# One hybrid decoder layer on one core: the second MLP product as seven block products instead of eight

## The chip, the core and the metric

The kernel runs on one core of one Trainium2 chip. The metric is the device time of one execution in microseconds (us), the median of several runs. Shorter is better.

## What is computed

One decoder layer over 2048 tokens of width 1024, in float32: an RMS norm, one input projection into three head groups (a gated causal convolution, a retention in chunks of 128 tokens, and dilated sliding-window attention), an output projection onto the residual, and an MLP. The change is in the MLP:

```python
x = x + mix.astype(x.dtype)
h2 = rms_norm(x, norm2_g)
ff = jnp.square(jax.nn.relu(h2 @ w_ff1.astype(F32))) @ w_ff2.astype(F32)
return x + ff.astype(x.dtype)
```

`w_ff1` is 1024 x 4096 and `w_ff2` 4096 x 1024. "The first MLP product" below is `h2 @ w_ff1`, "the second" the product with `w_ff2`.

## The kernel before

Everything is held transposed, channels on the 128 partitions and tokens along the free axis. The precision of float32 is kept by splitting each operand into a rounded part and a remainder: `halves` copies a 128x512 block into the rounded format on ScalarE and subtracts that from the original on VectorE. `mm3` then issues three matmuls of 128x512 for a pair of operands (rounded with rounded, rounded with remainder, remainder with rounded). Each operand lives in a unit of 4 KB per partition, from a pool with a fixed number of units: `wcp` (6, weights), `actp` (8, activations), `ur` (24), `ul` (8). Raw blocks land in `stage` (3 buffers).

The program's stages, by the time of the profiled execution: first projections with convolution and retention, then the attention's projections (to some 650 us); attention (to 920); output projection (to 1134); then the MLP twice, for tokens 0 to 1023 (H = 0, to 1808) and 1024 to 2047 (H = 1).

**First MLP product.** For each of 16 pairs of hidden rows (`pair`), seven block products of 12 matmuls each replace the eight that a 2 x 2 block product has (Winograd's form of Strassen's scheme: sums of weight blocks on GpSimd, `weight_sums`; sums of activation blocks on VectorE, made once; the block products collected in two PSUM banks and by VectorE). `pair` ends in the squared ReLU, two VectorE instructions of 128x1024, and two stores to `hid_d` in device memory.

**Second MLP product.** `group(g)` runs eight times per half, each over four hidden rows of 128: it loads four blocks of hidden and four of `w_ff2` (512 KB each) and splits them; then for each of 8 output blocks `d` and 2 token blocks `c` it sums 12 matmuls in one PSUM bank (`pso`), and VectorE adds the bank to `acc`. That is 8 x 16 x 12 = 1536 matmuls per half. While H = 0 does this, the operands of H = 1 for the first product are prepared (`next_half`).

**Order.** The program is written out in a nominal order, and a scheduler plays it through ahead of time and sets the order in which each engine's queue holds its instructions; an engine works its queue strictly in that order. Loads and stores go from SyncE's queue (SP), apart from the stores of the output projection, which go from GpSimd's (POOL).

**Around the change's other place**, the first projections: `conv_part(i)` and `retain(i)` for each 128-token chunk i give the matmuls. On GpSimd run the inverse roots (`rsqrt`: `rstd` per chunk, `rrr` per head, `rc` in the convolution), the gate product `rg` and `ro`, the retention's output times that gate. The path from a chunk's retention to PE goes: `rss` (VectorE), `rrr` (GpSimd), `rrr` x decay and `ro` (VectorE), `ro` x gate (GpSimd), transposes `ptr` (PE). The convolution's 31 taps are 248 VectorE instructions over 128x512 (`conv_chunk`), spread between these. GpSimd does nothing with `w_ff2` in this kernel.

## Time and profile before

| | |
|---|---|
| runs | 2489.5, 2485.09, 2488.97 us; median 2488.97 |
| profiled execution, its own time | 2485.31 us |
| span from first to last instruction | 2483.5 us |
| busy: PE, VectorE, ScalarE, GpSimd | 98%, 60%, 35%, 20% of the span |
| instructions: PE matmuls, VectorE, ScalarE, GpSimd | 12062, 2888, 1987, 363 |
| moved by DMA | 287.34 MB, mean 116 GB/s |
| chain that ended last | PE 88%, DVE 5%, DMA 3% |

PE is TensorE, DVE VectorE, ACT ScalarE, POOL GpSimd, SP SyncE's queue. Where an engine's busy time in a stretch equals the stretch, nothing on it waits there; a matmul's length in the profile overlaps the next one's, so the spacing of matmuls is the length of a stretch divided by their count. The chain of waits says the same in another way: it is followed back from the last instruction, and the engine that holds most of it sets the time.

### The profile page before, as it was taken

How to read it: one execution, taken by the hardware profiler on the slowest of the kernel's cores; microseconds unless marked ns; L12 is line 12 of the kernel's file. 1: busy time of each engine (PE TensorE's matmuls, PEld its weight loads, DVE VectorE, ACT ScalarE, POOL GpSimd, SP SyncE). 2: the span in 40 equal slices, each digit the busy share in tenths (PEclk: the TensorE clock that was granted, in tenths of full speed). 3: DMA queues.
4: the chain of work that ended last, by engine and by line, in shares of the span. 5: the costliest groups of instructions: out<-in, count | busy, mean ns of one | idle time of the engine just before them, and what ended most of it. 6: DMA issues, size and time to landing. Idle time of an engine off the chain costs nothing.

```text
span 2483.5 us, 32837 instructions
## 1 busy us (share of the span) xinstructions
PE 2434.3 (98%) x12062; PEld 2019.5 (81%) x12062; DVE 1478.2 (60%) x2888; ACT 873.0 (35%) x1987; POOL 504.1 (20%) x363
## 2 busy tenths in 40 slices
PE   7999999999999999999999999999999999999999
PEld 7878888999877776878888888888878888888887
DVE  5586787764476865675655565445575556644542
ACT  6433325333566674443222322112142223321210
POOL 0232211233122423344222200000132321000000
PEclk9999999999898999999999999999999999999999
DMA  7422104342352538552323363243132223632311
GB/s 217 133 64 73 38 19 117 95 115 84 97 107 77 115 84 286 188 179 101 126 103 110 111 229 124 80 152 111 68 114 107 102 104 134 234 106 68 119 68 68
DMA packets 192014, 287.34 MB, mean 116 GB/s; under 512 B 40317, under 2 KB 129516, under 8 KB 191852
## 3 DMA queue, kind: packets, MB, share of 16 engines
q1 hardware_dynamic: 189292, 276.85, 34.9%
q0 software_dynamic: 2560, 8.39, 0.9%
q8 instruction: 95, 1.56, 0.3%
q14 instruction: 67, 0.55, 0.1%
HBM read 213.19 MB, written 71.99 MB: 115 GB/s over the span
## 4 chain that ended last, share of the span: by engine, by line
PE 88%; DVE 5%; DMA 3%; ACT 1%; issue 1%; POOL 1%; SPq 0%; ACTq 0%; DVEq 0%; POOLq 0%
PE pso L917 29%; PE ps L158 16%; PE psy L917 11%; PE psz L917 7%; PE psx L917 7%; PE psc L917 6%; PE po L712 2%; PE sp L665 2%; PE pt L691 2%; PE sp L666 2%; DMA xn<-x 1%; PE rsp L350 1%; PE rpo L365 1%; DMA xs<-xT 1%; PE pb L167 1%
## 5 line engine op out<-in xcount | busy, mean ns | idle before, releaser
L917 PE MATMUL pso<-hid,w2a 128*128 128x512 f32 x1536 | 361.6, 395 | 0.0
L917 PE MATMUL pso<-hid,w2b 128*128 128x512 f32 x1536 | 361.1, 395 | 0.0
L917 PEld LDWEIGHTS pso<-hid,w2b 128*128 128x128 f32 x1536 | 288.0, 188 | 70.2
L917 PEld LDWEIGHTS pso<-hid,w2a 128*128 128x128 f32 x1536 | 288.0, 188 | 70.2
L929 DVE TENSOR_TENSOR acc<-acc,pso 128x512 f32<-128x512 f32 x256 | 174.4, 684 | 275.9 <-PE pso L917 275.3
L158 PE MATMUL ps<-whi,hh 128*128 128x384 f32 (+1 forms) x896 | 313.4, 351 | 12.5 <-ACT whi L117 9.4
L158 PE MATMUL ps<-whi,hl 128*128 128x384 f32 (+1 forms) x896 | 314.8, 351 | 0.3 <-DVE hl L150 0.3
L158 PE MATMUL ps<-wlo,hh 128*128 128x384 f32 (+1 forms) x896 | 311.8, 348 | 0.0
L929 POOL TENSOR_TENSOR s<-w1raw 128x512 f32<-128x512 f32 x64 | 93.8, 1485 | 758.3 <-DMA w1raw<-w_ff 693.0
L917 PE MATMUL psy<-T,S 128*128 128x512 f32 x768 | 192.4, 396 | 0.6 <-DVE S L619 0.5
L917 PE MATMUL psx<-B,A 128*128 128x512 f32 x768 | 191.8, 395 | 0.0
L158 PEld LDWEIGHTS ps<-whi,hh 128*128 128x128 f32 x896 | 169.3, 189 | 24.1 <-ACT whi L117 9.4
L158 PEld LDWEIGHTS ps<-whi,hl 128*128 128x128 f32 x896 | 169.3, 189 | 12.0 <-issue 5.4
L158 PEld LDWEIGHTS ps<-wlo,hh 128*128 128x128 f32 x896 | 169.3, 189 | 9.6 <-issue 3.1
L217 DVE SCALAR_TENSOR_TENSOR acc<-cbuf,cwt,acc 128x512 f32<-128x512 f32 x240 | 175.4, 776 | 0.2
L917 PEld LDWEIGHTS psy<-T,S 128*128 128x128 f32 x768 | 143.9, 188 | 36.2 <-DVE S L619 1.0
L917 PEld LDWEIGHTS psx<-B,A 128*128 128x128 f32 x768 | 144.1, 188 | 34.8
L917 PE MATMUL psc<-mix,wohi 128*128 128x512 f32 x512 | 164.0, 401 | 5.1 <-ACT wohi L641 2.7
L619 DVE TENSOR_TENSOR S<-s,S 128x512 fp32r<-128x512 f32 x128 | 109.2, 857 | 68.7 <-ACT S L617 68.1
L676 ACT ACTIVATE lt<-lt,ml 128x256 f32<-128x256 f32 (+1 forms) x288 | 129.2, 452 | 28.8 <-DVE ml L673 28.2
L617 ACT ACTIVATE S<-s 128x512 fp32r<-128x512 f32 x128 | 79.9, 628 | 164.1 <-PE psy L917 96.6
L617 ACT ACTIVATE hid<-hidraw 128x512 fp32r<-128x512 f32 x128 | 74.3, 626 | 164.6 <-DMA hidraw<-hid_d 116.2
(188 smaller groups left out, 3914.9 us busy)
## 6 DMA issues: line engine op xcount, KB each, us to landing
w1raw<-w_ff SPq DMA_DIRECT2D x66, 512.0 KB, 3.3
hidraw<-hid_d SPq DMA_DIRECT2D x64, 512.0 KB, 4.3
w2raw<-w_ff SPq DMA_DIRECT2D x64, 512.0 KB, 3.3
woraw<-w_out SPq DMA_DIRECT2D x33, 512.0 KB, 4.2
hid_d<-hidB SPq DMA_DIRECT2D x32, 512.0 KB, 2.7
hid_d<-hidA SPq DMA_DIRECT2D x32, 512.0 KB, 2.7
xs<-xT SPq DMA_DIRECT2D x31, 512.0 KB, 4.1
qkraw<-qkT_d SPq DMA_DIRECT2D x48, 256.0 KB, 4.8
```

The lines of the kernel that those rows point to most:

```text
L158: nc.tensor.matmul(ps, a[:, k, :], b[k][:], start=(k == 0 and m == 0), stop=(k == KT - 1 and m == 2))
L167: nc.tensor.matmul(pb[:, :TW], rb[:, h0 + u:h0 + u + 1].to_broadcast([33, P]), bands[:], start=True, stop=True)
L217: nc.vector.scalar_tensor_tensor(out=accs[j], in0=src, scalar=cwt[:, j, w:w + 1], in1=accs[j], op0=ALU.mult, op1=ALU.add)
L617: nc.scalar.activation(out=u[:, 0, :], in_=raw, func=AF.Copy)
L619: sub.tensor_tensor(out=u[:, 1, :], in0=raw, in1=u[:, 0, :].bitcast(F32), op=ALU.subtract)
L665: nc.tensor.matmul(sp[:, c0:c0 + n], qs[h][:, qsl], khi[h][:, ksl], start=True, stop=False)
L666: nc.tensor.matmul(sp[:, c0:c0 + n], qs[h][:, qsl], klo[h][:, ksl], start=False, stop=True)
L676: last_exp[0] = nc.scalar.activation(out=lt[:, :n], in_=lt[:, :n], func=AF.Exp, scale=-1.0, bias=mls[u][:, h:h + 1], accum_out=mls[u][:, 2 ...
L691: nc.tensor.transpose(pts[u][:, q * P:(q + 1) * P], lts[h, u][:, c * P:(c + 1) * P], ident[:])
L712: nc.tensor.matmul(po[h * 64:(h + 1) * 64, u0 * P:(u0 + n) * P], vt[:, kv, h * 64:(h + 1) * 64], mv, start=(one or i == 0), stop=(one or i ...
L917: nc.tensor.matmul(ps, w[a], act[b], start=(first and m == 0), stop=(last and m == 2), skip_group_check=more)
L929: eng.tensor_tensor(out=out, in0=a, in1=b, op=op)
```

## The change

The second product is taken through the same seven-product form. `pair` makes, after the squared ReLU (now on ScalarE: ReLU and square apart), the four sums of hidden blocks that the form needs, and stores seven blocks of 128x512 per pair instead of four. The sums of `w_ff2`'s blocks depend on nothing but the input: `w2_sums(j)` makes them on GpSimd during the first projections, for twelve of 16 pairs in the loop over retention chunks and for four in the loop of the attention's projections, and stores them in `w2s_d`. The seven products then run one after the other, each over all 16 pairs, accumulated in four PSUM banks (`pso`, four output blocks `d` at once); of eight banks four belong to either of two chains of sums, and VectorE adds a bank to `acc` once per product instead of once per group. The operands of each step (one block of weights and one of hidden, 256 KB each) are loaded and split anew for each product.

```diff
+    def w2_sums(j):
+        ra, rb = [stage.tile([P, 2, 512], F32, tag="raw", name=n) for n in ("w2sa", "w2sb")]
+        for u, t in enumerate((ra, rb)):
+            f = 2 * j + u
+            nc.sync.dma_start(out=t[:], in_=w_ff2[f * P:(f + 1) * P, :].rearrange("p (h c) -> p h c", h=2))
+        for out, a, b, op in ((rb[:, 1], ra[:, 1], rb[:, 1], ALU.add), (ra[:, 1], ra[:, 0], ra[:, 1], ALU.subtract),
+                              (ra[:, 0], rb[:, 1], ra[:, 0], ALU.subtract),
+                              (rb[:, 0], rb[:, 0], ra[:, 0], ALU.subtract)):
+            nc.gpsimd.tensor_tensor(out=out, in0=a, in1=b, op=op)
+        for u, t in enumerate((ra, rb)):
+            nc.sync.dma_start(out=w2s_d[j][u][:], in_=t[:])
...
         if 4 <= i < 7:
             bias_bands(i - 4)
+        w2_sums(i - 2)
...
+        if i % 2 == 0 and i <= 8:
+            w2_sums(NP - 5 + i // 2)
...
+    def norm_rows(H, c):
+        r = tp.tile([P, CH], F32, tag="ssum", name="rows")
+        nc.scalar.activation(out=r[:], in_=rows_of(H, c)[:], func=AF.Copy)
+        return r
...
-            for t, f in ((et, 2 * j + 1), (dt, 2 * j)):
-                nc.vector.scalar_tensor_tensor(out=t[:], in0=t[:], scalar=0.0, in1=t[:], op0=ALU.max, op1=ALU.mult)
-                nc.sync.dma_start(out=hid_d[f][:].rearrange("p (c t) -> p c t", c=2), in_=t[:])
+            for t in (et[:], dt[:, 1, :]):
+                nc.scalar.activation(out=t, in_=t, func=AF.Relu)
+            for t in (et, dt):
+                nc.scalar.activation(out=t[:], in_=t[:], func=AF.Square)
+            t12 = unit4(ur, "u", "t12", F32)
+            nc.sync.dma_start(out=hid_d[H][j][1][:], in_=et[:])
+            tt(nc.vector, t12[:, 0, :], dt[:, 1, :], dt[:, 0, :], ALU.subtract)
+            tt(nc.vector, t12[:, 1, :], et[:, 1, :], t12[:, 0, :], ALU.subtract)
+            tt(nc.vector, dt[:, 1, :], et[:, 1, :], dt[:, 1, :], ALU.subtract)
+            nc.sync.dma_start(out=hid_d[H][j][0][:], in_=dt[:])
+            nc.sync.dma_start(out=hid_d[H][j][2][:], in_=t12[:])
+            tt(nc.vector, et[:, 0, :], et[:, 0, :], t12[:, 1, :], ALU.subtract)
+            nc.sync.dma_start(out=hid_d[H][j][3][:], in_=et[:, 0:1, :])
...
+        steps = {} if H else {(3, 8): load_next, (4, 2): lambda: normalise(1, 0), (4, 8): lambda: normalise(1, 1),
+                              (5, 6): left_next, **{(6, 9 + kp): lambda kp=kp: act_sums(1, kp) for kp in range(4)}}
+        steps[0, 6] = load_acc
+        sb = banks(("mm", "mm", "s", "s"))
+        zb = banks(("pt", "pt", "o", "c"))
+        for n, (an, bn, chain, dh, c, done) in enumerate((
+                ("A11", "B11", 0, 0, 0, False), ("A12", "B21", 1, 0, 0, True), ("S2", "T2", 0, 0, 1, False),
+                ("S1", "T1", 1, 4, 1, False), ("S3", "T3", 0, 4, 1, True), ("S4", "B22", 1, 0, 1, True),
+                ("A22", "T4", 0, 4, 0, True))):
+            if n == 3:
+                zb = banks(("pt", "pt", "o", "c"))
+            ps = zb if chain else sb
+            fresh = n in (0, 1, 3)
+            for j in range(NP):
+                pool, tag = (stage, "raw") if n == 0 and j < 7 else (ur, "u")
+                raw = pool.tile([P, 2, CH], F32, tag=tag, name="ffraw")
+                nc.sync.dma_start(out=raw[:, 0, :], in_=source(an, j))
+                nc.sync.dma_start(out=raw[:, 1, :], in_=source(bn, j))
+                ua, ub = unit4(wcp, "w", "w2"), unit4(actp, "act", "hid")
+                halves(raw[:, 0, :], ua)
+                halves(raw[:, 1, :], ub)
+                for d in range(4):
+                    mm3(ps[d][:], hl(ua, slice(d * P, (d + 1) * P)), hl(ub), fresh and j == 0, j == NP - 1, not fresh)
+                if (n, j) in steps:
+                    steps[n, j]()
+            for d in range(4):
+                t = acc[dh + d][:, c, :]
+                tt(nc.vector, t, t, ps[d][:], ALU.add)
```

Over the program the queues differ by these counts: 3072 `pso` matmuls become 2688; on DVE 256 adds to `acc` become 56, 256 remainders in the second product become 448, 64 squared ReLUs go and 128 subtractions come; ACT's 256 rounding copies become 448, and 128 ReLU and square instructions come, with two copies of `rows`; POOL gains 64 additions of 128x512; SP has 1321 transfers instead of 873.

**GpSimd's queue in the first projections**, from the output `ro` of retention chunk 7 to the root `rrr` of chunk 8 and just behind it. Before (`rg` is the gate of chunks 8 and 9):

```order
46 L393 TENSOR_TENSOR ro_2113<-ro_2113,rg_1968 128x384
47 L326 TENSOR_TENSOR rg_2189<-rg_2189,retg_378 128x384
48 L81 TENSOR_TENSOR rrr_2343<-rss_2339,power_150 128x6
49 L393 TENSOR_TENSOR ro_2346<-ro_2346,rg_2189 128x384
50 L326 TENSOR_TENSOR rg_2426<-rg_2426,retg_378 128x384
```

The same stretch, now to `rrr` of chunk 8 only (`w2sa` and `w2sb` are the two blocks of `w2_sums`):

```order
65 L407 TENSOR_TENSOR ro_2534<-ro_2534,rg_2377 128x384
66 L183 TENSOR_TENSOR w2sb_2112<-w2sa_2111,w2sb_2112 128x512
67 L183 TENSOR_TENSOR w2sa_2111<-w2sa_2111 128x512
68 L183 TENSOR_TENSOR w2sa_2111<-w2sb_2112,w2sa_2111 128x512
69 L183 TENSOR_TENSOR w2sb_2112<-w2sb_2112,w2sa_2111 128x512
70 L340 TENSOR_TENSOR rg_2624<-rg_2624,retg_506 128x384
71 L183 TENSOR_TENSOR w2sb_2343<-w2sa_2342,w2sb_2343 128x512
72 L183 TENSOR_TENSOR w2sa_2342<-w2sa_2342 128x512
73 L183 TENSOR_TENSOR w2sa_2342<-w2sb_2343,w2sa_2342 128x512
74 L183 TENSOR_TENSOR w2sb_2343<-w2sb_2343,w2sa_2342 128x512
75 L183 TENSOR_TENSOR w2sb_2590<-w2sa_2589,w2sb_2590 128x512
76 L83 TENSOR_TENSOR rrr_2778<-rss_2774,power_278 128x6
```

Nine additions stand ahead of that `rrr`; from there to chunk 9's `rrr` there are eleven more. The other 44 lie in groups of one to seven ahead of the roots of other chunks, twelve of them ahead of `rrr` of chunks 10 and 11, eight among chunks 0 to 2, and 16 from chunk 14 on, half of those among the roots `rq` of the attention's projections.

**PE's queue in the second product.** Before, 12 matmuls in a row go into one bank, with four different pairs of operands:

```order
5128 L917 MATMUL pso_14380<-hid_14251,w2a_14256 128x512 x3
5129 L917 MATMUL pso_14380<-hid_14267,w2a_14272 128x512 x3
5130 L917 MATMUL pso_14380<-hid_14283,w2a_14288 128x512 x3
5131 L917 MATMUL pso_14380<-hid_14299,w2a_14304 128x512 x3
5132 L917 MATMUL pso_14394<-hid_14248,w2a_14256 128x512 x3
```

Now each pair of operands feeds four banks, three matmuls each, and is then done with:

```order
5278 L934 MATMUL pso_14100<-hid_15512,w2_15511 128x512 x3
5279 L934 MATMUL pso_14101<-hid_15512,w2_15511 128x512 x3
5280 L934 MATMUL pso_14102<-hid_15512,w2_15511 128x512 x3
5281 L934 MATMUL pso_14103<-hid_15512,w2_15511 128x512 x3
5282 L934 MATMUL pso_14100<-hid_15533,w2_15532 128x512 x3
```

A step of the changed product is 12 matmuls on one pair of operands, where a group had 192 matmuls on its eight blocks.

**SP's queue in the changed second product**, with what each transfer waits for (`DMAHW0` to `DMAHW7` are the eight completion counters that SP's transfers take in turn, `DVE` is the remainder that frees the raw buffer):

```order
905 L1204 DMA ffraw_15910<-w2s_d2_1_245 128x512 [waits DMAHW1_49,DVE_49]
906 L1205 DMA ffraw_15910<-hid_d0_2_1_121 128x512 [waits DMAHW2_49]
907 L1204 DMA ffraw_15931<-w2s_d3_1_247 128x512 [waits DMAHW3_49,DVE_49]
908 L1205 DMA ffraw_15931<-hid_d0_3_1_125 128x512 [waits DMAHW4_49]
909 L1204 DMA ffraw_15952<-w2s_d4_1_249 128x512 [waits DMAHW5_49,DVE_49]
```

Two transfers of 256 KB serve one step, where one of 512 KB served a block for a whole group; each waits for the one eight places ahead of it.

## Rows read from the trace of the kernel before

**Rows 1.** The page, parts 1 and 2: busy time, and 40 slices of the span.

```profile
PE 2434.3 (98%) x12062; PEld 2019.5 (81%) x12062; DVE 1478.2 (60%) x2888; ACT 873.0 (35%) x1987; POOL 504.1 (20%) x363
...
PE   7999999999999999999999999999999999999999
```

**Rows 2.** Busy us by stretch: start:end, length, PE, PEld, DVE, ACT, POOL; clock, DMA, GB/s.

```profile
245.00:344.00 99.00, 99.00 (x598) 86.80 (x597) 76.75 (x158) 32.20 (x84) 23.86 (x14) 1.00 0.12 36
...
400.00:560.00 160.00, 157.50 (x963) 152.53 (x963) 111.11 (x190) 66.67 (x131) 46.30 (x27) 1.00 0.41 112
...
1150.00:1400.00 250.00, 250.00 (x1083) 202.21 (x1082) 144.07 (x183) 67.02 (x114) 73.12 (x53) 1.00 0.30 108
...
1400.00:1500.00 100.00, 100.00 (x431) 80.66 (x430) 61.89 (x91) 33.56 (x58) 5.08 (x4) 1.00 0.55 192
...
2150.00:2470.00 320.00, 320.00 (x1373) 257.25 (x1372) 138.89 (x213) 58.76 (x98) 0.00 (x0) 1.00 0.25 87
```

**Rows 3.** The page, part 5, the costliest groups: busy us, mean ns of one.

```profile
L917 PE MATMUL pso<-hid,w2a 128*128 128x512 f32 x1536 | 361.6, 395 | 0.0
...
L917 PE MATMUL pso<-hid,w2b 128*128 128x512 f32 x1536 | 361.1, 395 | 0.0
```

**Rows 4.** Timeline of PE: start us, length us, what, count.

```profile
1442.21 5.53 PE L917 MATMUL pso<-hid,w2a 128*128 128x512 f32 x23
...
1785.55 22.56 PE L917 MATMUL pso<-hid,w2b 128*128 128x512 f32 x96
```

**Rows 5.** Groups of instructions by form, DVE and ACT in the MLP.

```profile
L619 DVE TENSOR_TENSOR hid<-hidraw,hid 128x512 fp32r<-128x512 f32 x128 | 83.4, 687 | 56.4 <-ACT hid L617 55.9
...
L617 ACT ACTIVATE hid<-hidraw 128x512 fp32r<-128x512 f32 x128 | 74.3, 626 | 164.6 <-DMA hidraw<-hid_d 116.2 <-PE pso L917 47.6
...
L929 DVE TENSOR_TENSOR acc<-acc,pso 128x512 f32<-128x512 f32 x256 | 174.4, 684 | 275.9 <-PE pso L917 275.3
...
L619 DVE TENSOR_TENSOR T<-x,T 128x512 fp32r<-128x512 f32 x24 | 18.1, 771 | 6.7 <-ACT T L617 6.6
...
L929 DVE TENSOR_TENSOR x<-x,x 128x512 f32<-128x512 f32 x8 | 8.0, 1006 | 0.0
```

**Rows 6.** The same view: one of the two squared-ReLU groups, and ScalarE at 1024 columns.

```profile
L1099 DVE SCALAR_TENSOR_TENSOR hidB<-hidB 128x1024 f32<-128x1024 f32 x32 | 40.0, 1251 | 0.0
...
L149 ACT ACTIVATE hh<-xs 128x1024 fp32r<-128x1024 f32 x31 | 32.8, 1060 | 53.7 <-PE ps L158 50.1 <-DMA xs<-xT 3.6
```

**Rows 7.** Tile s (weight sums of the first MLP product): ns minimum/median/maximum.

```profile
L929 POOL TENSOR_TENSOR s<-w1raw x64: 1282/1292/9568, 1130.2 to 2080.1; 128x512 f32<-128x512 f32 x64
```

**Rows 8.** Timeline of POOL in the first projections.

```profile
139.23 8.41 POOL L326 TENSOR_TENSOR rg<-rg,retg 128x384 f32<-128x384 f32 x1 [4.75 <-DVE rg L325]
...
244.75 1.36 POOL L393 TENSOR_TENSOR ro<-ro,rg 128x384 f32<-128x384 f32 x1 [1.68 <-DVE ro L390]
...
251.53 7.10 POOL L326 TENSOR_TENSOR rg<-rg,retg 128x384 f32<-128x384 f32 x1 [5.42 <-DVE rg L325]
...
268.28 1.43 POOL L81 TENSOR_TENSOR rrr<-rss,power 128x6 f32<-128x6 f32 x1 [9.66 <-DVE rss L385]
...
273.39 1.36 POOL L393 TENSOR_TENSOR ro<-ro,rg 128x384 f32<-128x384 f32 x1 [3.68 <-DVE ro L390]
```

**Rows 9.** Timeline of DVE, and the causal convolution's line: ns minimum/median/maximum.

```profile
139.08 4.71 DVE L217 SCALAR_TENSOR_TENSOR acc<-cbuf,cwt,acc 128x512 f32<-128x512 f32 x7
...
146.70 1.00 DVE L351 TENSOR_TENSOR rsm<-rsp,causal 128x512 f32<-128x512 f32 x2
...
L217 DVE SCALAR_TENSOR_TENSOR acc<-cbuf,cwt,acc x240: 729/740/1779, 110.3 to 527.7; 128x512 f32<-128x512 f32 x120
```

**Rows 10.** Timeline of PE at the transposes of retention chunk 8.

```profile
278.29 0.49 PE L397 MATMUL ptr<-ident,ro 128*128 128x128 f32 x3
```

**Rows 11.** DMA issues: what, queue, count, KB each, median us to landing.

```profile
hidraw<-hid_d SPq DMA_DIRECT2D x64, 512.0 KB, 4.3
...
x<-x_d SPq DMA_DIRECT2D x8, 512.0 KB, 10.1
```

More of the change, by code (lines that the diff above doesn't have):

```diff
@@ L43 @@
 FIRST = 2
-GRP = 4
 CH = 512
@@ L63 @@
     x1_d = [[dram.tile([P, HALF], F32, name=f"x1_d{h}_{d}") for d in range(KT)] for h in range(2)]
-    hid_d = [dram.tile([P, HALF], F32, name=f"hid_d{f}") for f in range(NF)]
+    NP = NF // 2
+    hid_d = [[[dram.tile([P, 2, CH], F32, name=f"hid_d{h}_{j}_{n}") for n in range(3)] +
+              [dram.tile([P, 1, CH], F32, name=f"hid_d{h}_{j}_3")] for j in range(NP)] for h in range(2)]
+    w2s_d = [[dram.tile([P, 2, CH], F32, name=f"w2s_d{j}_{n}") for n in range(2)] for j in range(NP)]
     def load_const(src, shape, name):
@@ L940, in norm_sums, with rows_of @@
         rsqrt(rn[:, n:n + 4], ms[:], 4)
-    def normalise(H, c):
+    rows = []
+    def rows_of(H, c):
         pr = bank("pr2")
@@ L947, in normalise @@
                              start=True, stop=True)
+        return pr
+    def norm_rows(H, c):
+        r = tp.tile([P, CH], F32, tag="ssum", name="rows")
+        nc.scalar.activation(out=r[:], in_=rows_of(H, c)[:], func=AF.Copy)
+        return r
+    def normalise(H, c):
+        pr = rows[c] if H else rows_of(H, c)
         for k in range(KT):
@@ L1115 @@
                 norm_sums(1, 1)
+            if H == 0 and j == 1:
+                rows[:] = [norm_rows(1, c) for c in range(2)]
         acc = []
-        for d in range(KT):
-            t = unit4(ul, "v", f"acc{d}", F32)
-            nc.sync.dma_start(out=t[:], in_=x1_d[H][d][:].rearrange("p (c t) -> p c t", c=2))
-            acc.append(t)
-        def group(g):
-            hid, w2 = [], []
-            for f in range(g * GRP, (g + 1) * GRP):
-                raw = stage.tile([P, 2, CH], F32, tag="raw", name="hidraw")
-                nc.sync.dma_start(out=raw[:], in_=hid_d[f][:].rearrange("p (c t) -> p c t", c=2))
-                hid.append([])
-                for c in range(2):
-                    u = unit4(ur, "u", "hid")
-                    halves(raw[:, c, :], u)
-                    hid[-1].append(u)
-                raw = stage.tile([P, 2, CH], F32, tag="raw", name="w2raw")
-                nc.sync.dma_start(out=raw[:], in_=w_ff2[f * P:(f + 1) * P, :].rearrange("p (h c) -> p h c", h=2))
-                w2.append([])
-                for h in range(2):
-                    u = unit4(actp, "act", "w2a") if h == 0 else unit4(wcp, "w", "w2b")
-                    halves(raw[:, h, :], u)
-                    w2[-1].append(u)
-            for d in range(KT):
-                if H == 0:
-                    for step in next_half.get((g, d), ()):
-                        step()
-                ws = slice(d % 4 * P, (d % 4 + 1) * P)
-                for c in range(2):
-                    ps = bank("pso")
-                    for f in range(GRP):
-                        mm3(ps[:], hl(w2[f][d // 4], ws), hl(hid[f][c]), f == 0, f == GRP - 1)
-                    tt(nc.vector, acc[d][:, c, :], acc[d][:, c, :], ps[:], ALU.add)
-                    if g == NF // GRP - 1:
-                        nc.sync.dma_start(out=outT[d * P:(d + 1) * P, H * HALF + c * CH:H * HALF + (c + 1) * CH],
-                                          in_=acc[d][:, c, :])
@@ L1155, in load_next, with banks @@
+        def banks(tags):
+            return [psA.tile([P, CH], F32, tag=t, name="pso", bufs=1 if t in "oc" else 2) for t in tags]
         def load_next():
@@ L1158, in load_next, with left_next @@
                 nc.sync.dma_start(out=x1[1, d][:], in_=x1_d[1][d][:].rearrange("p (c t) -> p c t", c=2))
-        def sums_next():
+        def left_next():
             for kp in range(4):
-                act_sums(1, kp)
-        end = NF // GRP
-        next_half = {(end - 3, 7): [load_next], (end - 2, 1): [lambda: normalise(1, 0)],
-                     (end - 2, 4): [lambda: normalise(1, 1)], (end - 1, 0): [lambda: left_ops(1)]}
-        for g in range(end):
-            group(g)
+                for name, k in (("B11", kp), ("B21", kp + 4)):
+                    op_b(name, kp, x1[1, k][:, 0, :])
@@ new lines @@
+        steps = {} if H else {(3, 8): load_next, (4, 2): lambda: normalise(1, 0), (4, 8): lambda: normalise(1, 1),
[26 more added lines that the diff above has]
+                tt(nc.vector, t, t, ps[d][:], ALU.add)
+                if done:
+                    nc.sync.dma_start(out=outT[(dh + d) * P:(dh + d + 1) * P,
+                                               H * HALF + c * CH:H * HALF + (c + 1) * CH], in_=t)
@@ L1169 @@
         if H == 0:
-            sums_next()
             right_ops(1, ("T3", "T1", "T4", "B22"))
```

12 lines of the change are left out of this document (added).

## The prediction

> **What bounds the kernel now.** I read the page's busy shares first. PE is busy for 98% of the span and in 39 of 40 slices at nine tenths or more; DVE comes next with 60% [rows 1]. The reader is to see that only two things can move the time much: fewer matmuls, or a wait put in front of PE. Next come the stretches. In the first projections (245 to 344 us), the first MLP product (1150 to 1400) and the second (2150 to 2470), PE's busy time equals the stretch, at a granted clock of 1.00, the upper of its two levels, 2.4 GHz [rows 2]. So nothing is won in these stages by making DVE, ACT or a transfer shorter, and each of them has a margin that the change may use up. The last row gives the price of a matmul: 320 us over 1373 are 0.2331 us from one to the next. The groups say how many there are in the second product, 2 x 1536 [rows 3], and the timeline that they follow each other without a gap: 96 of them in 22.56 us, whose last 0.39 us are one matmul's own length, are 95 spacings of 0.233 us [rows 4].
>
> **What the change takes from PE.** Each of 2 halves has 7 products x 16 pairs x 12 matmuls = 1344 instead of 1536. 384 fewer at 0.2331 us are 89.5 us, all on the path that sets the end. The bounds are narrow: 0.2331 is the spacing where PE alone counts, and any wait is priced below.
>
> **The second product's feed.** A step is now 12 matmuls on one pair of operands: 12 x 0.2331 = 2.80 us, 224 steps in all. In these 2.80 us ACT must copy two blocks, 2 x 0.626 = 1.25 us, DVE make two remainders, 2 x 0.687 = 1.37 us, and per 16 steps add four banks at 0.684, which is 0.17 us a step [rows 5]. DVE is then at 1.54 of 2.80 us. The 192 additional remainders (132 us) and the 200 dropped bank additions (137 us) nearly cancel on DVE; ACT gains 192 x 0.626 = 120 us. All of it lies beside PE; if that cover went, each 0.1 us by which a step outlasts 2.80 us would cost 22 us. The transfers are 512 KB per step, 187 GB/s; 192 GB/s stand in the row of 1400 to 1500 us at a DMA share of 0.55 and a fully busy PE [rows 2]. I cost the feed at 0.
>
> **The first product's tail.** Per pair, DVE loses two squared ReLUs of 1.25 us [rows 6] and gets four subtractions, at most 1.006 us each by the dearest such row [rows 5]: 1.5 us more. ACT gets a ReLU and two squares over 1024 columns at 1.06 us [rows 6] and a ReLU over 512 at about 0.63 us [rows 5]: 3.8 us. A pair is 84 matmuls, 19.6 us. DVE has 58% of that stage and ACT 27% [rows 2], so they come to 12.8 and 9.1 of 19.6 us. They wait for the pair's last bank, and behind them in their queues stand operands of the next pair, which are made several products ahead in six weight units. Cost 0; without that cover ACT's part would be 32 x 3.8 = 122 us. The four stores per pair wait on these results in SP's queue, with the next pairs' loads behind them; a load that has a pair's 19.6 us to land hides a wait of a few microseconds.
>
> **The turn from H = 0 to H = 1.** In the last ten steps of H = 0 (28.0 us) DVE has 20 remainders (13.7 us), four bank additions (2.7), sixteen sums at up to 1.006 us (16.1) and some sixteen remainders for the next half at 0.771 us (12.3) [rows 5]: 44.8 us, 16.8 more than there is. Six weight units hold six steps, 16.8 us, that may have been prepared. So it is between 0 (all prepared) and 17 us (none). I take 3, near the lower end, since before that stretch DVE needs 1.54 of 2.80 us and can fill the units. The banks' change between products costs nothing: the product between two uses of a bank lasts 45 us and four bank additions 2.7 us. The output's last transfers are as before.
>
> **The weight sums beside the first projections.** Here is the price. 64 additions on GpSimd take 1.28 us each when nothing disturbs them [rows 7], 82 us together, in a stage where PE has no slack. GpSimd's queue also holds the retention's `rrr` and `ro`, on whose results DVE and then PE's transposes wait; nine additions now stand ahead of `rrr` of chunk 8 and eleven ahead of chunk 9's. In the trace GpSimd gets little done beside the convolution: `rg`, started at 139.23, lasts 8.41 us and another 7.10 us at 251.53, where `ro` takes 1.36 [rows 8]. The first began as DVE started a run of seven taps with both inputs in SBUF, and it ended at 147.64, while DVE worked on `rsm`, which reads PSUM; taps in turn reach 1779 ns against 740 in the median [rows 9]. So an addition waits for a gap on DVE and then holds DVE up, and where the gaps do not do, DVE stops at `rrr` until GpSimd has caught up. Between the end of `ro` of chunk 7 (246.1) and `rrr` of chunk 9, some 49 us, 20 additions need 25.6 us; DVE is idle for 22% there, 11 us [rows 2]; and from `ro`'s end at 274.75 to the transposes at 278.29 there are 3.5 us of slack [rows 8, 10]. That leaves 11 us on PE. The next 49 us with twelve additions (15.4 us) about break even, and the 16 late ones (20.5 us) meet 49 us of idle DVE in 400 to 560 [rows 2]. Bounds: 0, if all 82 us fall into idle time, and 82, if each addition holds PE up for its length. A gain I exclude, as nothing is taken from this stage. I take 10, the working just shown, less a little for DVE's instructions on PSUM.
>
> The Trainium skill (SBUF — State Buffer, Who interferes with whom) says that a GpSimd instruction that reads SBUF and a VectorE instruction with two SBUF inputs exclude each other, and the second to start is blocked until the first ends. The rows of `rg` and of the taps agree with it [rows 8, 9]. By that rule alone, without the idle time, it would be the upper end, 82 us, and 2481 us in all.
>
> **Sum**, against the profiled execution's own 2485.3 us: -89.5 + 10 + 3 = -76.5, so 2408.8 us. That execution lies 3.7 us under the median of the three runs; the median of the changed kernel may lie as far above its fastest, and I give 2410. A measurement of this kernel can tell about 0.2%, 5 us, from no change.
>
> **Rivals.** (1) *GpSimd's queue comes onto the path.* If the additions stall PE at most of the chunks and not at two, half of the 82 us is lost: 2485.3 - 89.5 + 41 + 3 = 2440 us; at most 2481. For it speak the stretched `rg` [rows 8] and that DVE, stopped at `rrr`, delays the next chunk's operands too; against it that DVE is idle for a fifth to a third of the stage [rows 2]. (2) *The feed becomes the bound, and the kernel slower than before.* SP's transfers take eight completion counters in turn, so at most eight are under way, which is four steps. A step then lasts a quarter of the time from issue to landing. It decides from 4 x 2.80 = 11.2 us on, and at 12.6 us (3.14 us a step, 224 x 0.34 = 76 us) the whole gain is gone. At 14 us: 224 x (3.50 - 2.80) = 157, so 2566 us. For it: the burst of eight loads `x<-x_d` landed after 10.1 us in the median, and by that a step would take 2.5 us. Against it: 4.3 us for `hidraw` with twice the bytes of a transfer [rows 11]. (3) *The removed matmuls do not save their time*, since a bank is left after three matmuls and no longer after twelve. 896 changes of bank at 50 ns would cost 45 us: 2454; at 100 ns it would be 2498 and slower. Against it: 23 matmuls at 1442.21 that go to four banks in turn by the order of the queue take 5.53 us, the same spacing [rows 4].
>
> **How the numbers follow.** The forecast has 0.80, with a range of its own from 2394 (no loss at all, 2396, and a fast run) to 2430 (21 us more than taken, from the lock or the turn). Rival 1 has 0.14, since the rows show the mechanism and only the amount is open; rivals 2 and 3 have 0.03 each. The range from 2393 to 2445 holds the first and the lower half of rival 1. Faster by over 0.2%: 0.80 + 0.13 of rival 1 + 0.02 of rival 3 = 0.95; within 0.2%: 0.02, the ends of rivals 1 and 3 that meet the old time; slower: 0.03, rival 2.
>
> **What would show it.** In the profile after: 2688 `pso` matmuls at 0.233 us and PE busy throughout the second product; transfers `ffraw` landing well under 11 us; POOL's additions at 1.28 us and up, many stretched; gaps on PE in 240 to 300 us, of some 10 us together, released by DVE or POOL, where there were none. The first product should start some 10 us later than before, and each second product last about 45 us less. It is wrong if the first product starts 30 us later or more, if PE waits for `ffraw` or its halves all through the second product, or if the spacing of `pso` exceeds 0.24 us.

## The result and the profile after

The changed kernel takes 2416.83 us (median of 4 runs, 2412.23 to 2425.44), the kernel before beside it 2487.76 (2485.09 to 2489.5): a ratio of 0.972, with a 95% interval from 0.9689 to 0.975. The forecast was 2410, range 2393 to 2445. The total held, but not by the sum that was written for it: the gain in the second product was larger than forecast, the loss in the first projections three times as large, and the two errors nearly cancel. The profiled execution took 2412.23 us (span 2410.1), 73.1 less than that of before.

The page of the kernel after, parts 1 and 2: busy us, and 40 slices.

```profile
PE 2340.6 (97%) x11678; PEld 1957.3 (81%) x11678; DVE 1529.0 (63%) x2944; ACT 1100.7 (46%) x2309; POOL 592.4 (25%) x427
...
PE   7999999998999999899999999999999999999999
```

It answers to [rows 1]. TensorE is still the bound, but two slices of PE have fallen to eight tenths, the tenth (542 to 602 us), in the projections, and the seventeenth (964 to 1024 us), in the output projection. The busy time by stretch of the kernel after (start:end, length, PE, PEld, DVE, ACT, POOL; clock, DMA, GB/s) shows where:

```profile
245.00:344.00 99.00, 91.45 (x507) 78.54 (x506) 82.38 (x122) 27.67 (x69) 65.64 (x39) 0.93 0.52 171
400.00:560.00 160.00, 151.43 (x903) 143.30 (x902) 133.53 (x214) 66.02 (x137) 66.61 (x37) 0.97 0.50 148
...
2100.00:2400.00 300.00, 300.00 (x1324) 248.31 (x1324) 157.61 (x246) 129.02 (x220) 0.00 (x0) 1.00 0.62 217
```

Against [rows 2], the stretch from 245 to 344 us has lost its full PE (507 matmuls instead of 598) and some of its clock: 0.93, so a part of it ran at the lower of the two levels, after gaps on PE. The second product is full: 300 of 300 us at 1.00, with 217 GB/s of transfers beside it. There the spacing has fallen. The timeline of PE of the kernel after, in the second product of H = 1 (start, length, count):

```profile
2199.68 206.43 PE L934 MATMUL pso<-hid,w 128*128 128x512 f32 x910
```

910 matmuls in 206.43 us, whose last 0.39 are one matmul's own length, are 0.2267 us apart; before it was 0.2331 [rows 2] to 0.233 [rows 4].

The starts of the stages' first and last matmuls, from the PE records of both traces, give the balance in us:

| stage | before | after | difference |
|---|---|---|---|
| start to the last `ps` (first projections) | 647.2 | 680.9 | +33.7 |
| to the first `psc` (rest of the attention) | 271.2 | 267.5 | -3.7 |
| to the first `psx` (output projection) | 216.3 | 220.1 | +3.8 |
| first product, H = 0 | 307.5 | 309.2 | +1.7 |
| second product, H = 0 | 365.5 | 310.1 | -55.4 |
| first product, H = 1 | 308.0 | 307.9 | -0.1 |
| second product, H = 1 | 363.7 | 310.0 | -53.7 |
| sum | 2479.4 | 2405.7 | -73.7 |

So -109.1 us in the second products (forecast -89.5) and some +34 ahead of the first product (forecast +10).

**Where the projections lose.** The tile w2sb of the kernel after (ns minimum/median/maximum), the convolution's line beside [rows 9], and one of the retention's:

```profile
L183 POOL TENSOR_TENSOR w2sb<-w2sa,w2sb x16: 1262/1300/5319, 53.8 to 549.3; 128x512 f32<-128x512 f32 x16
...
L231 DVE SCALAR_TENSOR_TENSOR acc<-cbuf,cwt,acc x240: 730/741/1819, 117.2 to 557.7; 128x512 f32<-128x512 f32 x120
...
L322 DVE TENSOR_TENSOR rqk<-rqk,rtmp x16: 541/554/1611, 38.6 to 422.7; 128x384 f32<-128x384 f32 x16
```

Part 5 of the page has the same 240 taps of 128x512 with their mean, 849 ns; in the trace of before the first 690 us give 776 for them. The timelines of POOL, DVE and PE of the kernel after show one such place:

```profile
297.93 5.32 POOL L183 TENSOR_TENSOR w2sb<-w2sa,w2sb 128x512 f32<-128x512 f32 x1 [5.15 <-DMA w2sb<-w_ff]
303.33 1.60 POOL L183 TENSOR_TENSOR w2sa<-w2sa 128x512 f32<-128x512 f32 x1
305.00 1.46 POOL L183 TENSOR_TENSOR w2sa<-w2sb,w2sa 128x512 f32<-128x512 f32 x1
```

```profile
295.58 5.38 DVE L231 SCALAR_TENSOR_TENSOR acc<-cbuf,cwt,acc 128x512 f32<-128x512 f32 x8
300.88 0.55 DVE L317 TENSOR_TENSOR rqk<-rraw,rt 128x384 f32<-128x384 f32 x1
...
302.02 1.78 DVE L231 SCALAR_TENSOR_TENSOR acc<-cbuf,cwt,acc 128x512 f32<-128x512 f32 x1
303.72 1.61 DVE L330 TENSOR_TENSOR rv<-rv,decay 128x384 f32<-128x384 f32 x1
305.26 1.61 DVE L322 TENSOR_TENSOR rqk<-rqk,rtmp 128x384 f32<-128x384 f32 x1
306.80 1.01 DVE L365 TENSOR_TENSOR rsm<-rsp,causal 128x512 f32<-128x512 f32 x2
```

```profile
303.43 0.39 PE L160 MATMUL ps<-whi,hh 128*128 128x512 f32 x1
307.53 2.82 PE L379 MATMUL rpo<-rv,rsm 128*128 128x64 f32 x12 [3.71 <-DVE rsm L365]
```

The first addition starts in DVE's run of taps and lasts 5.32 us, four times the shortest. From 302 us on the two engines slow each other: `rqk` from `rtmp` (L322), which takes DVE 0.554 us in the median, lasts 1.61 beside an addition. `rsm` comes late, and PE stands for 3.71 us. Another such gap, 6.46 us at 540.8, waits for DVE's `raw`; from 539.64 to 544.48 GpSimd runs three additions there, and two of DVE's taps last 3.44 us beside them, where one takes 0.741 in the median.

The waits of PE in the kernel after, from 100 us to the last `ps` (us in total, times, longest), show which engine was late:

```profile
PE ptq L536 <- DVE raw L526: 10.1, 4, 6.5
PE rpo L379 <- DVE rsm L365: 4.5, 2, 3.7
PE ps L160 <- ACT rv L329: 3.0, 1, 3.0
PE ptc L288 <- ACT rm L413: 2.1, 1, 2.1
PE ptr L345 <- ACT rm L413: 1.9, 1, 1.9
PE ptr L411 <- POOL ro L407: 1.7, 2, 0.9
PE rsp L364 <- ACT rqm L353: 0.2, 1, 0.2
```

They sum to 23.5 us, where the kernel before has 4.2. VectorE ended 14.6 us of them and GpSimd itself 1.7. VectorE lost time in two ways: its 240 taps took 17.5 us more, and it waited 17.6 us for GpSimd's `rrr` where it had waited 11.6.

### The profile page after: what moved, and what is told of

Read it like the earlier page. It is cut to its first block, busy times and chain, and to the rows that moved or that the text cites. A ratio compares the mean times of both kernels' runs of the same rounds, so it can differ in the third digit from the quotient of the medians.

```text
span 2410.1 us, 33394 instructions
## 1 busy us (share of the span) xinstructions
PE 2340.6 (97%) x11678; PEld 1957.3 (81%) x11678; DVE 1529.0 (63%) x2944; ACT 1100.7 (46%) x2309; POOL 592.4 (25%) x427
## 4 chain that ended last, share of the span: by engine, by line
PE 76%; DVE 11%; DMA 7%; POOL 2%; issue 2%; ACT 1%; SPq 1%; ACTq 0%; POOLq 0%; DVEq 0%
PE pso L934 25%; PE psy L934 11%; PE ps L160 10%; PE psx L934 7%; PE psz L934 7%; DVE acc L231 4%; PE psc L934 4%; PE po L729 2%; PE pt L708 2%; PE sp L682 2%; PE sp L683 2%; DMA xn<-x 2%; DMA ml_d<-ml 1%; DMA qkraw<-qkT_d 1%; DMA woraw<-w_out 1%
## 5 line engine op out<-in xcount | busy, mean ns | idle before, releaser
L934 PE MATMUL pso<-hid,w 128*128 128x512 f32 x2688 | 610.2, 389 | 0.0
L934 PEld LDWEIGHTS pso<-hid,w 128*128 128x128 f32 x2688 | 504.5, 188 | 105.1 <-ACT hid L634 0.2
L634 ACT ACTIVATE w<-ffraw 128x512 fp32r<-128x512 f32 x224 | 141.5, 632 | 310.0 <-PE pso L934 273.9
L636 DVE TENSOR_TENSOR w<-ffraw,w 128x512 fp32r<-128x512 f32 x224 | 155.9, 696 | 196.6 <-ACT w L634 195.7
L946 POOL TENSOR_TENSOR s<-w1raw 128x512 f32<-128x512 f32 x64 | 85.2, 1351 | 712.8 <-PE pso L934 322.2
L231 DVE SCALAR_TENSOR_TENSOR acc<-cbuf,cwt,acc 128x512 f32<-128x512 f32 x240 | 192.1, 849 | 0.2
L636 DVE TENSOR_TENSOR hid<-ffraw,hid 128x512 fp32r<-128x512 f32 x224 | 152.7, 685 | 6.2 <-ACT hid L634 4.9
L634 ACT ACTIVATE hid<-ffraw 128x512 fp32r<-128x512 f32 x224 | 137.2, 618 | 6.7 <-DMA ffraw<-hid_d 6.4
L634 ACT ACTIVATE A<-w1raw 128x512 fp32r<-128x512 f32 x96 | 60.1, 628 | 170.6 <-PE psy L934 126.7
```

What stands on the lines that cost most here:

```text
L231: nc.vector.scalar_tensor_tensor(out=accs[j], in0=src, scalar=cwt[:, j, w:w + 1], in1=accs[j], op0=ALU.mult, op1=ALU.add)
L634: nc.scalar.activation(out=u[:, 0, :], in_=raw, func=AF.Copy)
L636: sub.tensor_tensor(out=u[:, 1, :], in0=raw, in1=u[:, 0, :].bitcast(F32), op=ALU.subtract)
L934: nc.tensor.matmul(ps, w[a], act[b], start=(first and m == 0), stop=(last and m == 2), skip_group_check=more)
L946: eng.tensor_tensor(out=out, in0=a, in1=b, op=op)
```

## The experiments

Three questions were open: is it the additions on GpSimd that cost the 34 us (and not their loads, stores and buffers, or a new order); why did the spacing of matmuls fall; and can the loss be had back.

**Without the additions.** In `w2_sums` the loop over the four additions is taken out; the second product then works with plain copies of the weights.

```
-        for out, a, b, op in (...):
-            nc.gpsimd.tensor_tensor(out=out, in0=a, in1=b, op=op)
```

> The changed kernel with the 64 GpSimd additions of w2_sums left out: the 32 loads of w_ff2, the stage buffers and the 32 stores stay, so that the stored sums are plain copies of the weights and the second MLP product works with them. The output projection's first matmul (psc) began at 918.4 us in the kernel before and at 948.4 in the changed one, a loss of 30.0. Theory 1, the additions are the cost (GpSimd and DVE slow each other, and what waits for GpSimd comes late): psc begins near 920 (917 to 925) and the time is about 2383 us. Rival, the loads, stores and stage buffers are the cost: psc stays at 945 to 950 and the time at 2412. Second rival, the new order that the scheduler gives the projections is the cost, and any kernel with extra work there gets one: psc somewhere between, with gaps on TensorE in other places than in the changed kernel.

Measured: 2387.56 us, psc at 920.5, the taps' mean 780 ns. The loss in the projections is gone although the loads and stores are still there.

**The additions alone.** Loads and stores of `w2_sums` are taken out, and the additions read a constant tile `wz`; S1 to S4 of the second product are read from hidden tiles.

```
-            nc.sync.dma_start(out=t[:], in_=w_ff2[f * P:(f + 1) * P, :]...)
...
+            nc.gpsimd.tensor_tensor(out=out, in0=wz[:], in1=wz[:], op=op)
...
-            nc.sync.dma_start(out=w2s_d[j][u][:], in_=t[:])
```

> The changed kernel with the loads and stores of w2_sums left out: the same 64 GpSimd additions of 128x512 at the same places, but reading a constant tile, into the same stage buffers; S1 to S4 of the second MLP product are then read from the hidden tiles, so that its loads keep their number and size. Theory 1, the additions are the cost: psc begins at 945 to 950, time about 2412 us. Between: the additions wait for their loads on GpSimd's queue (34.3 us in the changed kernel) and hold what stands behind them, so that both are needed: psc begins at 925 to 940 and the time is near 2398. Rival, loads, stores and stage buffers alone: psc at 917 to 925, time about 2383.

Measured: 2412.16 us, psc at 948.2, last `ps` at 685.3, taps 841 ns. The whole loss is there without any load; that the additions waited 34.3 us for their loads in the changed kernel cost nothing more.

**Half of each addition.** Each works on 256 of 512 columns; the other half of the sums is plain copies.

```
-            nc.gpsimd.tensor_tensor(out=out, in0=a, in1=b, op=op)
+            nc.gpsimd.tensor_tensor(out=out[:, 0:256], in0=a[:, 0:256], in1=b[:, 0:256], op=op)
```

> The changed kernel with each of the 64 GpSimd additions of w2_sums working on 256 of its 512 columns; the other half of the stored sums is plain copies. With all columns the last projection matmul (ps) came at 680.9 us, with no additions at 652.4, in the kernel before at 647.2; the output projection's first (psc) at 948.4, 920.5 and 918.4. Theory 1, the time that GpSimd works sets the loss (its own queue is late and VectorE is slowed while it works): the loss halves, last ps at 664 to 670, psc at 930 to 938, about 2398 us. Rival, it is the number of additions on GpSimd's queue with their waits, or the order that they bring with them: last ps at 676 or later, psc at 944 or later, 2408 us or more. Second rival, only the excess over some free time of GpSimd costs: last ps at 658 or before, 2392 us or less.

Measured: 2404.59 us, last ps at 671.4, psc at 941.0: a little past the range of theory 1, and 4.6 us short of 676, where the first rival begins (the number of the additions, or the order that they bring). The groups of POOL in the first 690 us of this run (busy us, mean ns of one) say why more than half is left: one of the four has 1360 ns and the others 891 to 900, where the changed kernel has 1477 to 1625. Two of them:

```profile
L183 POOL TENSOR_TENSOR w2sb<-w2sa,w2sb 128x256 f32<-128x256 f32 x16 | 21.8, 1360 | 97.5 <-DMA w2sb<-w_ff 73.8 <-DMA band_d<-bt 17.8 <-DMA mix_d<-rm 4.7
...
L183 POOL TENSOR_TENSOR w2sa<-w2sa 128x256 f32<-128x256 f32 x16 | 14.4, 900 | 1.1
```

**The additions on VectorE.**

```
-            nc.gpsimd.tensor_tensor(out=out, in0=a, in1=b, op=op)
+            nc.vector.tensor_tensor(out=out, in0=a, in1=b, op=op)
```

> The changed kernel with the 64 additions of w2_sums on VectorE in place of GpSimd, all else the same. VectorE is 64% busy in the first 690 us of the kernel before, and 64 additions of about 0.69 us (the row of such a tile in the MLP) are 44 us more, 71%. Theory 1a, the loss comes from two engines slowing each other and from a slow queue on GpSimd: it goes for the larger part, psc begins at 920 to 930, 2387 to 2397 us. Rival 1b, the loss comes from VectorE being late for TensorE, whoever takes its time: VectorE now loses 44 us where GpSimd's sharing cost it about 35, psc begins at 945 to 955 and the time is 2410 to 2420.

Measured: 2407.36 us, psc at 943.9, last ps at 665.8. That lies between the two theories and nearer to rival 1b: VectorE has not the room either, but it does the work in 45.6 us (683 to 739 ns each) where GpSimd needs 97.7. The taps are back at 778 ns. Of the way from last ps to psc, this run took 278.1 us and the changed kernel 267.5, at a granted clock of 0.85 against 0.92 in 690 to 915 us, where neither has additions; so the last `ps` is the better measure of the loss.

The last `ps`, in the changed kernel and all its variants, beside the time that the additions occupied their engine in the first 690 us (the sum of four groups):

| additions in the projections | busy us | last `ps` at us | loss |
|---|---|---|---|
| none (five kernels: the one without additions and four below) | 0 | 651.2 to 653.7, mean 652.3 | 0 |
| on VectorE | 45.6 | 665.8 | 13.5 |
| on GpSimd, 256 columns | 64.8 | 671.4 | 19.1 |
| on GpSimd (changed kernel, the two with hidden tiles in ur below, the additions alone) | 97.2 to 99.1 | 680.9, 686.0, 676.7, 685.3, mean 682.2 | 29.9 |

13.5/45.6, 19.1/64.8 and 29.9/98.2 are each about 0.30 us lost per us of additions. The first three kernels of the last row agree here in what their engines do and still spread by 9 us, so that a single run above is good to some 5 us: that the additions bring the loss is shown, and that it grows with the time that they hold an engine fits every row, but the steps between the rows are single runs and the exact proportion is not shown. Nor is the order taken apart from the additions: the scheduler gave the runs on VectorE, on 256 columns and with the additions alone an order each, other than the changed kernel's. The five changed kernels without additions stand 5 us behind the 647.2 of the kernel before (649.6 in the run of it with exchanged pools, below). Four of them have no work of the change in this stage at all, and on every engine their instructions come in the order of the kernel before up to 640 us; so for these four it is neither the change's transfers nor the order, but a spread from one run to another.

**The sums beside the first MLP product.** Sum j is formed in pair j of H = 0, its buffers from ur.

```
-        w2_sums(i - 2)
...
+            if H == 0:
+                w2_sums(j)
```

> The changed kernel with w2_sums taken out of the projections: sum j is formed beside channel pair j of the first MLP product of the first half, with its two buffers from ur (4 of whose 24 units are free there) in place of stage. Theory 1 (and the rivals that blame anything in the projections): psc begins near 918, the 30 us come back, and the first product has room for 4 more GpSimd additions per pair (GpSimd is 25% busy over the whole kernel): 2383 us, 2378 to 2392, if first-product pairs stay at 20 us each. Rival, the cost goes with the work: the first product's pairs lengthen by 1 to 2 us each in the first half and the time stays at 2400 to 2415.

Measured: 2402.77 us, ratio 0.9641 [0.9595, 0.9686]. The time is the rival's, but not for its reason: the first product of H = 0 takes 309.2 us, as in the changed kernel. The projections are as hoped (psc at 924.9), and 18 us go again at the turn to the second product, which takes 328.5 us in H = 0. The timeline of PE of this run:

```profile
1485.56 23.90 PE L931 MATMUL pso<-hid,w 128*128 128x512 f32 x96 [8.41 <-ACT hid L631]
1514.75 5.62 PE L931 MATMUL pso<-hid,w 128*128 128x512 f32 x13 [5.30 <-ACT hid L631]
```

At that turn SP issues the loads of the last sum, and only behind them the next operands of the second product.

**Three of the sums later.**

```
-            if H == 0:
+            if H == 0 and j < 13:
                 w2_sums(j)
...
+            steps.update({k: lambda j=j: w2_sums(j) for k, j in (((0, 10), 13), ((0, 14), 14), ((1, 2), 15))})
```

> The moved sums again, but only those of pairs 0 to 12 beside the first MLP product; 13, 14 and 15 are formed inside the second product (after its steps (0, 10), (0, 14) and (1, 2)), which needs the first of them from its third block on. In the run with all sums beside the first product the two gaps of 8.4 and 5.3 us at the turn to the second product stood behind the loads of the last sum on SP, and that product's first half took 328.5 us against 310. Theory: without these the gaps go, the first half's second product takes 310 to 312 us, 2385 us (2380 to 2392), 30 below the changed kernel. Rival, the gaps come from the crowded units of ur (w2sa, w2sb and t12 beside 20 units of operands) and stay: 2398 to 2405.

Measured: 2387.26 us, ratio 0.9584 [0.9561, 0.9608], whose interval lies wholly under the changed kernel's: the fastest version of all, with nothing left out. The second product of H = 0 takes 311.8 us, its gaps at the turn are 0.43 and 0.35. The busy time by stretch of this run, in the projections and in the first MLP product with the sums beside it:

```profile
245.00:344.00 99.00, 99.00 (x598) 86.77 (x597) 75.15 (x152) 31.82 (x83) 25.26 (x14) 1.00 0.14 40
1160.00:1440.00 280.00, 280.00 (x1220) 226.71 (x1219) 169.54 (x231) 128.59 (x187) 155.63 (x109) 1.00 0.67 244
```

GpSimd is busy there for 155.63 of 280 us, 56%, which is between its 66% of 245 to 344 us and its 42% of 400 to 560 us in the changed kernel, and PE is busy throughout. The same additions, of 1341 to 1550 ns in the mean, are free where DVE prepares its operands several products ahead, and cost 29 us where PE waits for DVE's last result chunk by chunk. DVE also has more room there: it was busy for 58% of 1150 to 1400 us before the change and for 78% of 245 to 344 [rows 2]. Which of the two differences makes the additions free was not tried apart.

**The place of the moving operand.** Now the spacing. In both traces the matmuls at 0.227 to 0.230 us are those whose moving operand lies in actp or ul, and those at 0.233 those whose moving operand lies in ur.

```
-                pool, tag = (stage, "raw") if n == 0 and j < 7 else (ur, "u")
+                pool, tag = (stage, "raw") if n == 0 and j < 7 else (actp, "act")
...
-                ua, ub = unit4(wcp, "w", "w2"), unit4(actp, "act", "hid")
+                ua, ub = unit4(wcp, "w", "w2"), unit4(ur, "u", "hid")
```

> The changed kernel with one swap in the second MLP product: the moving operand's rounded halves (hid) come from the pool ur in place of actp, the raw tiles after the first seven from actp in place of ur. Theory, the place of the moving operand sets the distance between matmuls: pso goes from 226.7 ns back to 233.4 ns, 2688 x 6.7 ns = 18 us longer, 2430 us. Rival, the distance fell because the same moving operand is used for four banks in a row: 226.7 ns stays, and the time stays at 2412 (within 5 us).

Measured: 2459.03 us. The spacing did what the theory said (the timeline row stands below): the way through four banks is not the reason. The time rose by 28 us more than that: 8.8 are lost ahead of the first product, where this kernel does the same as the changed one (the spread named above), and some 20 at the two turns to the second product, where `pso` waits for its first halves. The raw tiles now stand in actp beside the first product's results; that this is why was not tried.

**The exchange in the kernel before.**

```
-                    u = unit4(ur, "u", "hid")
+                    u = unit4(actp, "act", "hid") if c == 0 else unit4(ur, "u", "hid")
...
-                    u = unit4(actp, "act", "w2a") if h == 0 else unit4(wcp, "w", "w2b")
+                    u = unit4(ur, "u", "w2a") if h == 0 else unit4(wcp, "w", "w2b")
```

> The kernel before with one exchange in its second MLP product: the hidden tiles of the first half of the columns (c = 0) are rounded into actp in place of ur, and w2a into ur in place of actp; the number of tiles in each pool stays. Theory, the place of the moving operand sets the distance: the pso matmuls with c = 0 (half of 3072) go from 233.4 to about 227 ns and those with c = 1 stay at 233.4, 1536 x 6.6 ns = 10 us: 2476 us, ratio 0.996. Rival, the distance belongs to the way the changed kernel works through its banks (four in turn, each left after 3 matmuls): all pso matmuls stay at 233.4 ns, and the time at 2486.

Measured: 2482.29 us, ratio 0.9972 [0.9951, 0.9994]. Here the theory fell in the form that it had. With each of the 3072 records joined to the pools of its operands by the kernel's order on PE, the distance from one to the next is

```
moving in  stationary in   count   mean ns
actp       ur (w2a)          766     233.3
actp       wcp (w2b)         767     229.4
ur         ur (w2a)          749     228.7
ur         wcp (w2b)         752     233.6
```

So neither operand's place decides by itself. It is slower when one lies in ur and the other does not: 1516 matmuls at 4 to 5 ns less are 6.6 us, and the ratio gives 7. By the kernel's allocation actp, wcp and ul lie between 32 and 120 KB of a partition, ur between 128 and 224.

**Both operands in ur.** The run with the hidden tiles in ur, and one line more:

```
-                ua, ub = unit4(wcp, "w", "w2"), unit4(ur, "u", "hid")
+                ua, ub = unit4(ur, "u", "w2"), unit4(ur, "u", "hid")
```

> The run with the hidden tiles in ur, and the weights' rounded halves w2 in ur too (raw tiles after the first seven from actp as there), so that both operands of the second MLP product lie in ur. In the run of the kernel before with the exchanged pools, matmuls whose two operands lay in the same part of the memory (both in ur, or both in actp and wcp) came 226.7 to 229.7 ns apart and those with one in each 233 to 234. Theory, it is whether the two operands lie on the same side: pso goes back to 227 to 229 ns, 2688 x 5 to 6.6 ns = 13 to 18 us under the run with hid alone in ur: 2441 to 2446 us. Rival, the moving operand's place alone: 233.4 ns, 2459 us.

Measured: 2445.16 us. The timelines of PE of the second product of H = 1, first with hid alone in ur, then with both:

```profile
2199.69 220.66 PE L934 MATMUL pso<-hid,w 128*128 128x512 f32 x945
```

```profile
2199.75 220.48 PE L934 MATMUL pso<-hid,w 128*128 128x512 f32 x972
```

(220.66 - 0.39)/944 is 0.2333 us, (220.48 - 0.39)/971 is 0.2267. The theory of the two sides holds, in the spacing and in the time.

**The same in the first product, twice.** Its moving operands B and T2, T3 lie in ur, its stationary ones in wcp. First T3 and B22 go to actp, and hidA, hidB, s12 and s34 to ur:

```
-        u = unit4(ul, "v", name) if name in ("T1", "T4") else unit4(ur, "u", name)
+        if name in ("T1", "T4"):
+            u = unit4(ul, "v", name)
+        else:
+            u = unit4(actp, "act", name) if name in ("T3", "B22") else unit4(ur, "u", name)
```

> As the run sent with it (13 sums beside the first MLP product, 3 in the second), and in the first MLP product 8 tiles exchange pools: the moving operands T3 and B22 are rounded into actp in place of ur, and the products' and weight sums' tiles (hidA, hidB, s12, s34) lie in ur in place of actp. Theory, the moving operand's place sets the distance in the first product too: the matmuls with T3 and B22 go from 233.4 to about 227 ns, 24 of 84 per pair, 768 x 6.6 ns = 5 us, so 5 us below the other run, 2380 us. Rival, the distance in the first product has another reason (what DVE, ACT and GpSimd do beside it): 233.4 ns stays and the time is the same or, since T3 and B22 now wait for actp's units at the turns, 2 to 10 us longer.

Measured: 2598.33 us, ratio 1.0429 [1.0397, 1.0461], slower than anything else. The timeline of PE of this run:

```profile
1317.90 2.91 PE L931 MATMUL psy<-T,A 128*128 128x512 f32 x12
1320.64 2.88 PE L931 MATMUL psz<-B,S 128*128 128x512 f32 x12
1327.06 1.06 PE L931 MATMUL psy<-T,S 128*128 128x512 f32 x2 [3.53 <-ACT S L631]
```

The 12 matmuls with B22 take 2.88 us, (2.88 - 0.39)/11 = 0.226 a step, against 2.97 in the changed kernel: the spacing fell as forecast. But nearly every pair has a gap of some 3.5 us, 105 us in all, in which the halves of S2 stand in ACT's queue behind the previous pair's ReLU, and the granted clock in this product was 0.90 in H = 0 (1160 to 1440 us) and 0.87 in H = 1 (1900 to 2200). The reverse, stationary halves to ur from the third pair on:

```
-            u = unit4(wcp, "w", name)
+            u = unit4(ur, "u", name) if right else unit4(wcp, "w", name)
```

> As the run with 13 sums beside the first MLP product and 3 in the second (2387 us), and in the first product, from its third pair on, the stationary halves of A11, A12, S2, S3 and S4, whose moving operands lie in ur, are rounded into ur in place of wcp; t12, w2sa and w2sb go to wcp in their place. S1 and A22, whose moving operands lie in ul, stay in wcp. Theory, operands on the same side: 60 of the 84 matmuls of a pair go from 233.4 to about 227 ns, 28 pairs x 60 x 6.6 ns = 11 us: 2376 us (2370 to 2382). Rival, the four units that are left in ur for the stationary halves (six in wcp) are too few, or the new order lets a halving wait behind other work on ACT, as in the run that moved T3 and B22: the spacing falls but TensorE waits 1 us or more per pair, 2390 us or more.

Measured: 2456.76 us, ratio 0.9869 [0.9846, 0.9892]: the rival's case. The matmuls with both operands in ur stood 227.8 ns apart (1463 of them), those that still had one in wcp 233.4; the 11 us were there to be had, and the waits took them seven times over. The largest is this, at the turn, in the timeline of PE of this run:

```profile
1509.06 3.35 PE L931 MATMUL pso<-hid,w 128*128 128x512 f32 x7 [15.74 <-ACT hid L631]
```

ACT itself stood for 17.53 us before it, until a load of `ffraw` had landed. That too few units of ur were left for these loads was expected, but not tried apart from the new order.

## Why the prediction was right, and where not

**The bound** held: TensorE is busy for 97%, and the large changes are in its matmuls' count and spacing, in waits ahead of them and in its clock.

**384 matmuls fewer, -89.5 us: under-sized, -109.1.** The count was right. The step that failed is "The bounds are narrow: 0.2331 is the spacing where PE alone counts". It was the spacing for hidden tiles in ur and weights in actp or wcp, and the change put both into actp and wcp. 384 x 0.2331 are 89.5, and 2688 x (0.2331 - 0.2267) are 17 more; that makes 106.7 of the 109.1. The trace of before had shown it, in matmuls with T4 and T1 (in ul) at 229 to 230 ns in the mean beside 233.4 for B in ur, and I read one stage's spacing only. Two rows of its timeline of PE, 12 matmuls with T4 and 12 with B22:

```profile
1311.01 2.91 PE L917 MATMUL psy<-T,A 128*128 128x512 f32 x12
1313.75 2.97 PE L917 MATMUL psz<-B,S 128*128 128x512 f32 x12
```


**The feed at 0** held: transfers landed in 4.0 to 5.3 us in the median, far from the 11.2 at which rival 2 begins. DMA issues of the kernel after (count, KB each, median us to landing), the answer to [rows 11]:

```profile
ffraw<-hid_d SPq DMA_DIRECT2D x224, 256.0 KB, 5.2
...
ffraw<-w2s_d SPq DMA_DIRECT2D x128, 256.0 KB, 4.0
ffraw<-w_ff SPq DMA_DIRECT2D x96, 256.0 KB, 5.3
```

**The first product's tail at 0** held: 307.5 became 309.2 us in H = 0 and 308.0 became 307.9 in H = 1. **The turn at 3** was nearly nothing; the timeline of PE of the kernel after has one gap there, 0.87 us, where before there was one of 0.52:

```profile
1808.63 2.97 PE L934 MATMUL psy<-T,A 128*128 128x512 f32 x12 [0.87 <-DVE hidB L946]
```

**The weight sums at +10: mis-sized, 29 of the 34 us that were lost ahead of the first product.** The mechanism was the one read from [rows 8, 9], and its bounds of 0 to 82 held it. What failed is the step from DVE's idle time to PE: "11 us on PE" for two chunks, "about break even" for the next 49 us, and nothing for the 16 late additions that "meet 49 us of idle DVE in 400 to 560". Against the kernel before, the same projection matmul came 19 us later at 341 us, 25 at 486 and 33 at 567: each of these parts paid, the last one too. As I read it, idle time of DVE is no store that an addition may use up. It is there while PE works on the products for DVE's next input; when additions slow DVE or hold back `rrr`, DVE is late for that input, and PE waits although DVE is idle for a sixth of the stretch (82.38 of 99 us busy). How much of the 29 us each of these two ways cost was not tried apart. A gap on PE then costs twice, since the clock falls: in 245 to 344 us PE stood for 7.55 us, but 91 matmuls are missing, 15 us at the 0.1656 us of [rows 2]. By my own test, the first product 30 us later or more, this part was wrong (33.8), and rival 1 came nearest to what happened. Its 2440 us did not come about, since it took the 89.5 for the gain.

The Trainium skill (SBUF — State Buffer, Who interferes with whom) says that a VectorE instruction with two SBUF inputs and a GpSimd instruction that reads SBUF contend for an exclusive lock. The taps agree with it: 849 ns with the additions on GpSimd, 778 with them on VectorE. By that rule alone, as the prediction priced it, 82 us would be lost; the 29 us agree with neither that sum nor mine.

**The sum.** -109.1 + 33.8 + 1.7 - 0.1 = -73.7; forecast -76.5. It was right by two errors, of -20 and +24 us, and so by luck. Rival 3 is refuted by the spacing.

## What to carry to other kernels

Take the price of a removed instruction from the operands that the changed kernel will give it, not from the stage it leaves: tiles that change pools can change the price. Work for an idle engine was free here in a stage whose operands are made well ahead and where VectorE has room, and was paid for where TensorE waits for VectorE chunk by chunk: choose the stage by what the other engines owe TensorE there, and not by the idle time of the engine that gets the work. When a total comes out as forecast, check each term by its stage, for two wrong ones can meet.

## What the runs showed that I had not expected

A matmul of 128x512 with its weights came every 0.2267 to 0.230 us when the moving and the stationary operand lay both in the lower pools (32 to 120 KB of a partition) or both in ur (128 to 224 KB), and every 0.2333 to 0.2336 us when they lay on different sides. Which border counts was not tried, and why the kernel before with the exchange had 228.7 and 229.4 ns, where the changed kernel had 226.7, is open. And kernels that do the same in the first projections spread by 9 us there from one run to another (676.7 to 686.0), more than the five without additions (651.2 to 653.7).
